# Transposing the token-major SwiGLU blocks: on TensorE, or by DMA in two planes of 16-bit halves

## The chip, the cores and the metric

One core of a Trainium2 chip runs the kernel. The metric is the device time of one execution in microseconds (us), taken as the median of several runs. A profile of one execution stands beside it.

The engines that matter here: PE (TensorE) for matmuls and transposes, ACT (ScalarE), DVE (VectorE), SP (SyncE), which issues nearly all DMAs, and the DMA queue behind SP. Every engine works through its own instructions in order.

## The reference, cut to what matters

```
def _swiglu(t, w_gate, w_up, w_down):
    return (jax.nn.silu(t @ w_gate) * (t @ w_up)) @ w_down

for l in range(DEPTH):                                  # DEPTH = 2
    f = _swiglu(_rmsnorm(h, ffn1_pre_g[l]), ffn1_w_gate[l], ffn1_w_up[l], ffn1_w_down[l])
    h = h + 0.5 * _rmsnorm(f, ffn1_post_g[l])
    ...                                                 # three attentions, gated and merged
    f = _swiglu(_rmsnorm(h, ffn2_pre_g[l]), ffn2_w_gate[l], ffn2_w_up[l], ffn2_w_down[l])
    h = h + 0.5 * _rmsnorm(f, ffn2_post_g[l])
```

The input `x` is 1 x 512 x 1024 in float32; the hidden width `D_FF` is 2816, 22 tiles of 128. So there are four SwiGLU layers, named a0, c0, a1 and c1 in the kernel (a and c are the first and second of a decoder layer).

## The kernel before

Every float32 factor is split into a high and a low part (`split`: an ACT cast makes `wh`, a DVE subtraction makes `wl`), and a product is three matmuls (`mm3`, L202 to L206): high by high, high by low, low by high.

Of the 22 hidden tiles 16 lie in two chunks (`ci`) of 8 tiles. For each chunk, gate and up are computed in `token_products`, as a product of 2 x 2 blocks that needs seven smaller products instead of eight (`n`, in the order 0, 2, 1, 3, 4, 5, 6). In these, tokens are the output's partitions ("token-major"): `token_product` has the activations as the stationary operand and weights of 512 columns as the moving one, four steps `kk` of two groups of three matmuls, 24 matmuls of 128x512. The down products of a chunk (`products`, `product`) are of the same kind, with the hidden values as activations, and these must have the hidden dimension in the partitions. So the finished blocks of the hidden values have to be transposed.

A block of gate times up is finished after the up products n = 1, 4, 5 and 6; it is 128 tokens by 1024 values (two groups of tokens by 512 hidden values). `turn` transposes it in the product that follows, at its step `kk` 2: eight PE transposes of 128x128 into two PSUM banks (L800), and two ACT copies of 128x512 out of them (L802) into the rows of `hr`, which `hidden_rows` gives. That makes 4 blocks x 2 chunks x 4 layers = 32 turns.

`PLAN` (L1635) writes the order of the products of a layer out by hand: seven gate products of chunk 0 (G0), a slot, seven up products (U0), seven gate products of chunk 1 (G1), seven up products (U1), then the fourteen down products with the plain hidden tiles 18 to 21 (`gates`, `ups`) between them. So turns fall in two places of a layer: where U0 goes over into G1, and where U1 goes over into the down products.

Other steps that the prediction follows:

- the weights of a product come in two units of 128x1024 (two `kk` each): a fetch of 512 KB by SP (`BlockUnit.fetch`, issue L296), for some products a DVE difference of two blocks (L326), the ACT cast (L181) and the DVE low part (L182); the `wh` and `wl` rings have four buffers each, which is two products;
- `first_factor` makes the split activations `aha`, `ala` of a down product from `hr`, with differences of its blocks in `asa`;
- evictions of a token product out of PSUM: L775 (ACT) for n = 2 and 3, L777 and L779 (DVE) for the others; L746 (ACT) carries the sum of n = 0 over to the banks of n = 1 before that product begins;
- `tmp` gives a [128, 512] float32 tile from a ring of five buffers (`f32t`), and the tag `rs` has one buffer of [128, 1024] float32.

The tile framework orders the instructions of each engine and sets the waits; `tc.keep_in_program_order` ties an instruction to its place among the others that are tied on its engine.

Of the kernel before, what the change touches and what calls it, by code (L numbers as in the profile page):

```python
# [9 lines left out]
F32 = mybir.dt.float32  # L10
F32R = mybir.dt.float32r
BF16 = mybir.dt.bfloat16
AF = mybir.ActivationFunctionType
ALU = mybir.AluOpType
AX = mybir.AxisListType
# [2 lines left out]
P = 128  # L18
# [4 lines left out]
def kernel(  # L23
# [38 lines left out]
    nc = tc.nc  # L62
    _, S, D = x.shape
# [3 lines left out]
    ND = D // P  # L67
# [7 lines left out]
    FC = 8  # L75
# [12 lines left out]
    ident = cst.tile([P, P], F32, name="ident")  # L88
    make_identity(nc, ident)
    ident16 = cst.tile([P, P], BF16, name="ident16")  # L90
    eps_t = cst.tile([P, 1], F32, name="eps_t")
    nc.vector.memset(eps_t[:], D * EPS)
    one_t = cst.tile([P, 1], F32, name="one_t")
    nc.vector.memset(one_t[:], 1.0)
    causal16 = cst.tile([P, P], BF16, name="causal16")
    sel = cst.tile([104, NH], F32, name="sel")

    def tmp(name):
        return sb.tile([P, S], F32, tag="f32t", bufs=5, name=name)
# [3 lines left out]
    def stile(shape, tag, name, dt=F32R):  # L103
        return sb.tile(shape, dt, tag=tag, bufs=BUFS[tag], name=name)
# [4 lines left out]
    def pbank(tag, name):  # L109
        return ps.tile([P, S], F32, tag=tag, bufs=4, name=name)  # L110
# [67 lines left out]
    def split(h_ap, l_ap, src, scale=None, later=False):  # L178
# [4 lines left out]
        else:  # L183
            both = [nc.scalar.activation(h_ap, src, AF.Copy, scale=scale)]  # L184
            make = lambda: nc.vector.scalar_tensor_tensor(l_ap, src, scale, h_ap.bitcast(F32), ALU.mult, ALU.subtract)  # L185
# [7 lines left out]
    def sigmoid_neg(t, z, c):  # L193

        b, minus = nbgate[:, c[0], c[1]:c[1] + 1], bgate[:, c[0], c[1]:c[1] + 1]
        nc.scalar.activation(t, z, AF.Abs, bias=b)
        nc.scalar.activation(t, t, AF.Exp, scale=-1.0)
        nc.scalar.activation(t, t, AF.Ln, bias=one_t[:])  # L198
        nc.vector.scalar_tensor_tensor(t, z, minus, t, ALU.max, ALU.add)  # L199
        nc.scalar.activation(t, t, AF.Exp, scale=-1.0, bias=minus)  # L200

    def mm3(pt, lh, ll, rh, rl, start, stop, free=False):  # L202

        nc.tensor.matmul(pt, lh, rh, start=start, stop=False, skip_group_check=free)  # L204
        nc.tensor.matmul(pt, lh, rl, start=False, stop=False, skip_group_check=free)  # L205
        nc.tensor.matmul(pt, ll, rh, start=False, stop=stop, skip_group_check=free)  # L206
# [271 lines left out]
    def rstd(st, a, b=None):  # L478

        s, m, y, w = st[:, a:a + 1], st[:, 3:4], st[:, 4:5], st[:, 5:6]  # L480
        if b is None:
            nc.scalar.activation(y, s, AF.Ln, bias=eps_t[:])
            nc.vector.tensor_scalar(m, s, D * EPS, None, ALU.add)
# [118 lines left out]
    def ffn(l, src, wg, wu, wd, dst, name, spare, parked, plan, aside=None):  # L602
# [4 lines left out]


        hid, st = {}, {}
        hr = {}  # L610
        f0 = NC * FC
        tags = ["q"] * 2 + ["o"] * 4
        act = lambda k, c=FULL: quad_act(src.us)(k, c)
# [1 line left out]
        def hidden_rows(i):  # L615
            if i not in hr:
                hr[i] = stile([P, FC // 2, S], ("k", "tri")[i // 2], f"hr{name}_{i}", F32)
            return hr[i]
# [114 lines left out]
        def in_product(n):  # L733
            if n in (0, 1, 6):
                i, j = ((0, 0), (0, 1), None, None, None, None, (1, 1))[n]
                return [block(i, j, part) for part in range(2)]
            return st["u", n]

        def token_product(ci, up, n, uns):

            nm = f"{name}{'gu'[up]}_{ci}_{n}"
            if n in (0, 1, 2):
                st["c", n] = [pbank("z" if n == 0 else "mm", f"pw{nm}_{e}") for e in range(2)]
            if n == 1:
                for e in range(2):
                    nc.scalar.copy(st["c", 1][e][:], st["c", 0][e][:])  # L746
            if n == 0:
                if not up:
                    st["s", ci] = {}
            pts = st["c", SUM[n]]  # L750
            h, l = in_product(n)
            opens, ends = n in (0, 2), n in (1, 4, 6)
            for un in uns:
                for k in range(un.nk):
                    kk = un.k0 + k
                    for e in range(2):
                        c = slice(e * P, (e + 1) * P)
                        mm3(pts[e][:], h[:, kk, c], l[:, kk, c], un.h[:, k], un.l[:, k], opens and kk == 0,
                            ends and kk == ND // 2 - 1, free=True)
                        yield 3 * S * PE_US  # L760
                    if kk == ND // 2 - 2:
                        yield from turn("z")
            if n == 0:
                return
            q = TO[n]
            g = st["s", ci]
            if not up and q not in g:
                g[q] = stile([P, FC // 2, S // 2], "f", f"s{name}_{ci}_{q[0]}{q[1]}", F32)[:]
            g = g[q]
            r = hidden_rows(2 * ci + q[1])[:, :, HALVES[q[0]]] if up else g  # L770
            for e in range(2):
                p = pts[e][:].rearrange("p (f q) -> p f q", f=2)
                re, ge = r[:, 2 * e:2 * e + 2], g[:, 2 * e:2 * e + 2]
                if n in (2, 3):
                    nc.scalar.copy(re, p)  # L775
                elif n in (4, 5):
                    nc.vector.tensor_tensor(re, re, p, ALU.add)  # L777
                elif up:
                    nc.vector.tensor_tensor(ge, p, ge, ALU.mult)  # L779
                else:  # L780
                    nc.scalar.activation(re, p, AF.Silu)
            if n in (4, 5):
                if up:
                    nc.vector.tensor_tensor(g, r, g, ALU.mult)
                else:
                    nc.scalar.activation(r, r, AF.Silu)
            if up and n in (1, 4, 5, 6):
                st["turn"] = (f"{nm}", g, r)

        def turn(tag):  # L790

            nm, g, r = st.pop("turn", (None, None, None))
            if nm is None:
                return
            g = g.rearrange("p f q -> p (f q)")
            for b in range(2):
                pt = pbank(tag, f"ht{nm}_{b}")
                for f in range(2):
                    for e in range(2):
                        nc.tensor.transpose(pt[:, (2 * f + e) * P:(2 * f + e + 1) * P],  # L800
                                            g[:, e * S + (2 * b + f) * P:][:, :P], ident[:])
                nc.scalar.copy(r[:, 2 * b:2 * b + 2], pt[:].rearrange("p (f q) -> p f q", f=2))  # L802
                yield 0.4

        def token_products(ci, up):

# [37 lines left out]
        def product(ci, n, uns):  # L844
            if n == 0 and ci == 0:
                RINGS["o"] = 2
                dst.begin()
            if n < 6:
                first_factor(ci, n + 1)
            if n in (0, 1, 2):  # L850
                st["b", SUM[n]] = [pbank("z", f"pd{name}_{ci}_{n}_{e}") for e in range(2)]
            pts = st["b", SUM[n]]
            if n == 1 and ci:
                for e in range(2):
                    nc.scalar.copy(pts[e][:], dst.fs[e][:, HF[0]])
            h, l = st["a", ci, n]
            opens, ends = n in (0, 2) or (n == 1 and not ci), n in (1, 4, 6)
            for un in uns:
                for k in range(un.nk):
                    kk = un.k0 + k  # L860
                    for e in range(2):
                        c = slice(e * P, (e + 1) * P)
                        mm3(pts[e][:], h[:, kk, c], l[:, kk, c], un.h[:, k], un.l[:, k], opens and kk == 0,
                            ends and kk == FC // 2 - 1, free=True)
                        yield 3 * S * PE_US
                    if kk == FC // 2 - 2:
                        yield from turn("mm")
            if n == 0:
                return
            i, hf = TO[n]  # L870
            for e in range(2):
                f = dst.fs[2 * i + e][:, HF[hf]]
                if n == 1:
                    nc.scalar.copy(f, st["b", 0][e][:])
                    nc.vector.tensor_tensor(f, f, pts[e][:], ALU.add)
                elif ci == 0 and n in (2, 3, 6):
                    nc.scalar.copy(f, pts[e][:])
                else:
                    nc.vector.tensor_tensor(f, f, pts[e][:], ALU.add)
# [767 lines left out]

    wps, wsb = pbank("z", "warm"), tmp("warm").bitcast(BF16)
    nc.vector.memset(wsb[:, 0:S], 0.0)
    mc = None  # L1650
    for l in LAYERS:
        i, mn = 3 * l, []
# [44 lines left out]
```

## Time and profile before

| | |
|---|---|
| median of 3 runs | 2390.12 us (2388.59 to 2391.15) |
| the profiled execution's own time | 2389.31 us |
| its span in the profile | 2387.6 us |
| granted TensorE clock, mean | 0.998 |
| PE busy | 2370.0 us |
| DVE busy | 1844.2 us |
| ACT busy | 1425.1 us |
| GpSimd busy | 75.1 us |
| DMA, mean | 142 GB/s |

Busy time is the time in which an engine has an instruction in work. Matmuls are pipelined and their ends are modelled, so a busy PE is not the same as PE at its peak. In a group of instructions, the figures behind the count are busy time in us and the mean duration of one in ns; behind the second bar stands the idle time just before them and what ended it. In a timeline line the first number is the start in us from the start of the span, the second the length. In a view of windows each engine has its busy time in the stretch, with the number of its instructions, then come the granted clock, the busy share of the DMA engines and their rate.

### The profile page before, as it was taken

To read this page: it belongs to the slowest core of one execution; us is meant where nothing else is said; L and a number is where in the kernel's file an instruction comes from. 1 tells how busy PE (TensorE), PEld (TensorE's weight loads), DVE (VectorE), ACT (ScalarE), POOL (GpSimd) and SP (SyncE) were. 2 spreads that over 40 slices of the span, in tenths; PEclk is the share of its full clock that TensorE was granted. 3 is DMA by queue.
4 is the path that set the end of the run, shared out by engine and by line. 5 is a ranking of instruction groups with operands and counts; after the bars stand their busy time and mean duration, and the time that the engine had idled before them with its cause. 6 is when DMAs were issued, how large, how long until landed. Compare 5 with 4: busy or idle time off the path is not lost.

```text
span 2387.6 us, 31555 instructions
## 1 busy us (share of the span) xinstructions
PE 2370.0 (99%) x11975; PEld 2006.6 (84%) x11975; DVE 1844.2 (77%) x2414; ACT 1425.1 (60%) x2250; POOL 75.1 (3%) x134
## 2 busy tenths in 40 slices
PE   9999999999999999999999999999999999999998
PEld 7888889888888888888888888888888888888887
DVE  8878877577777688788788788766777767887885
ACT  6655555576766555555655554656777664655554
POOL 1000000000111000000000000000001100000000
PEclk9999999999999999999999999999999999999999
DMA  6554455223323655444645554542323235555444
GB/s 205 184 150 158 142 189 147 80 82 87 89 72 106 195 175 175 144 158 157 206 140 167 150 176 156 187 116 71 98 71 97 80 115 198 164 176 154 154 140 153
DMA packets 232173, 338.23 MB, mean 142 GB/s; under 512 B 10683, under 2 KB 125395, under 8 KB 232021
## 3 DMA queue, kind: packets, MB, share of 16 engines
q1 hardware_dynamic: 231924, 336.18, 44.3%
q8 instruction: 94, 1.54, 0.3%
q14 instruction: 59, 0.48, 0.1%
q0 software_dynamic: 96, 0.03, 0.0%
HBM read 319.39 MB, written 16.78 MB: 141 GB/s over the span
## 4 chain that ended last, share of the span: by engine, by line
PE 89%; DVE 5%; DMA 3%; ACT 2%; issue 1%; SPq 0%; POOL 0%; DVEq 0%; ACTq 0%
PE pg L205 3%; PE pg L204 3%; PE pg L206 3%; PE pda L205 3%; PE pda L206 3%; PE pda L204 3%; PE pdc L205 3%; PE pdc L206 2%; PE pdc L204 2%; PE pb L206 1%; PE pb L205 1%; PE pb L204 1%; PE pq L205 1%; PE pq L204 1%; PE pq L206 1%
## 5 line engine op out<-in xcount | busy, mean ns | idle before, releaser
L204 PE MATMUL pg<-us_a,wh_wg 128*128 128x512 f32 x384 | 150.9, 393 | 0.0
L205 PE MATMUL pg<-us_a,wh_wg 128*128 128x512 f32 x384 | 149.8, 390 | 0.0
L206 PE MATMUL pg<-us_a,wl_wg 128*128 128x512 f32 x384 | 149.7, 390 | 0.0
L205 PE MATMUL pda<-wl_da,aha 128*128 128x512 f32 x224 | 87.6, 391 | 0.6 <-DVE wl_da L182 0.5
L205 PE MATMUL pdc<-wl_dc,ahc 128*128 128x512 f32 x224 | 87.5, 391 | 0.3 <-DVE wl_dc L182 0.3
L204 PE MATMUL pda<-wh_da,aha 128*128 128x512 f32 x224 | 87.4, 390 | 0.0
L204 PE MATMUL pdc<-wh_dc,ahc 128*128 128x512 f32 x224 | 87.4, 390 | 0.0
L206 PE MATMUL pda<-wh_da,ala 128*128 128x512 f32 x224 | 87.2, 389 | 0.0
L206 PE MATMUL pdc<-wh_dc,alc 128*128 128x512 f32 x224 | 87.2, 389 | 0.0
L206 PEld LDWEIGHTS pg<-us_a,wl_wg 128*128 128x128 f32 x384 | 72.1, 188 | 15.2
L204 PEld LDWEIGHTS pg<-us_a,wh_wg 128*128 128x128 f32 x384 | 72.1, 188 | 14.1
L205 PEld LDWEIGHTS pg<-us_a,wh_wg 128*128 128x128 f32 x384 | 72.2, 188 | 14.1
L182 DVE TENSOR_TENSOR wl_dc<-raw_dc,wh_dc 128x1024 fp32r<-128x1024 f32 x50 | 61.1, 1223 | 29.3 <-ACT wh_dc L181 29.1
L181 ACT CAST wh_dc<-raw_dc 128x1024 fp32r<-128x1024 f32 x50 | 52.6, 1053 | 43.9 <-PE pdc L206 15.1
L182 DVE TENSOR_TENSOR wl_da<-raw_da,wh_da 128x1024 fp32r<-128x1024 f32 x50 | 61.1, 1223 | 22.3 <-ACT wh_da L181 22.0
L181 ACT CAST wh_da<-raw_da 128x1024 fp32r<-128x1024 f32 x50 | 52.7, 1055 | 39.3 <-PE pda L206 15.0
L185 DVE SCALAR_TENSOR_TENSOR wl_wg<-raw_wg,wh_wg 128x1024 fp32r<-128x1024 f32 x48 | 58.4, 1220 | 21.6 <-ACT wh_wg L184 21.6
L199 DVE SCALAR_TENSOR_TENSOR ga<-pg,bgate,ga 128x512 f32<-128x512 f32 x48 | 35.9, 747 | 49.5 <-ACT ga L198 49.5
L181 ACT CAST wh_uc<-raw_uc 128x1024 fp32r<-128x1024 f32 x44 | 46.3, 1053 | 43.5 <-PE pwc1u L206 10.3
L181 ACT CAST wh_ua<-raw_ua 128x1024 fp32r<-128x1024 f32 x44 | 46.2, 1053 | 34.3 <-PE pwa1u L206 10.3
L184 ACT ACTIVATE wh_wg<-raw_wg 128x1024 fp32r<-128x1024 f32 x48 | 50.5, 1057 | 24.0 <-PE pv L1088 11.7
L182 DVE TENSOR_TENSOR wl_uc<-raw_uc,wh_uc 128x1024 fp32r<-128x1024 f32 x44 | 53.7, 1220 | 14.3 <-ACT wh_uc L181 14.2
(655 smaller groups left out, 8044.4 us busy)
## 6 DMA issues: line engine op xcount, KB each, us to landing
raw_da<-in_ffn_w_down_dram SPq DMA_DIRECT2D x66, 512.0 KB, 4.6
raw_dc<-in_ffn_w_down_dram SPq DMA_DIRECT2D x66, 512.0 KB, 5.3
raw_ga<-in_ffn_w_gate_dram SPq DMA_DIRECT2D x52, 512.0 KB, 3.9
raw_ua<-in_ffn_w_up_dram SPq DMA_DIRECT2D x52, 512.0 KB, 3.9
raw_gc<-in_ffn_w_gate_dram SPq DMA_DIRECT2D x52, 512.0 KB, 3.8
raw_uc<-in_ffn_w_up_dram SPq DMA_DIRECT2D x52, 512.0 KB, 3.8
raw_wg<-in_w_gate_dram SPq DMA_DIRECT2D x48, 512.0 KB, 3.5
raw_wo<-in_w_out_dram SPq DMA_DIRECT2D x24, 512.0 KB, 3.6
```

The lines of the kernel that those rows point to most:

```text
L181: both = [nc.scalar.copy(h_ap, src)]
L182: make = lambda: nc.vector.tensor_tensor(l_ap, src, h_ap.bitcast(F32), ALU.subtract)
L184: both = [nc.scalar.activation(h_ap, src, AF.Copy, scale=scale)]
L185: make = lambda: nc.vector.scalar_tensor_tensor(l_ap, src, scale, h_ap.bitcast(F32), ALU.mult, ALU.subtract)
L199: nc.vector.scalar_tensor_tensor(t, z, minus, t, ALU.max, ALU.add)
L204: nc.tensor.matmul(pt, lh, rh, start=start, stop=False, skip_group_check=free)
L205: nc.tensor.matmul(pt, lh, rl, start=False, stop=False, skip_group_check=free)
L206: nc.tensor.matmul(pt, ll, rh, start=False, stop=stop, skip_group_check=free)
```

## The change

The turn of a block no longer uses PE. A float32 word is taken as two 16-bit halves:

- two ACT copies split the block's words into two planes of 128x1024 halves (`th`, both in `tmp` tiles), tied to step `kk` 1 of the product after the one that finished the block;
- two DMA transposes, issued by SP and tied to step `kk` 3 of the same product, turn each plane, in eight groups of 128 columns, into a plane `tr`. For the blocks n = 1 and 5 both planes lie in the one buffer of `rs`, for n = 4 and 6 in two `tmp` tiles;
- two ACT copies join the planes in `hr`, each writing every second half-word, tied to steps `kk` 0 and 1 of the third product after the one that finished the block (`age` 2).

The list `turns` holds the blocks that are under way; `token_product` and `product` call `turn(kk)` at each step.

```diff
+U16 = mybir.dt.uint16
...
-        hr = {}
+        hr, turns = {}, []
...
-                    if kk == ND // 2 - 2:
-                        yield from turn("z")
+                    turn(kk)
...
             if up and n in (1, 4, 5, 6):
-                st["turn"] = (f"{nm}", g, r)
-
-        def turn(tag):
-
-            nm, g, r = st.pop("turn", (None, None, None))
-            if nm is None:
-                return
-            g = g.rearrange("p f q -> p (f q)")
-            for b in range(2):
-                pt = pbank(tag, f"ht{nm}_{b}")
-                for f in range(2):
-                    for e in range(2):
-                        nc.tensor.transpose(pt[:, (2 * f + e) * P:(2 * f + e + 1) * P],
-                                            g[:, e * S + (2 * b + f) * P:][:, :P], ident[:])
-                nc.scalar.copy(r[:, 2 * b:2 * b + 2], pt[:].rearrange("p (f q) -> p f q", f=2))
-                yield 0.4
+                turns.append([nm, g, (2 * ci + q[1], q[0]), n in (1, 5), 0, None])
+
+        def turn(kk):
+
+            later = tc.keep_in_program_order
+            for one in turns:
+                nm, g, (row, i), own, age, planes = one
+                if kk == 1 and age == 0:
+                    one[5] = planes = [tmp(f"th{nm}_{h}")[:].bitcast(U16) for h in range(2)]
+                    words = g.rearrange("p f q -> p (f q)").bitcast(U16)
+                    for h, plane in enumerate(planes):
+                        later(nc.scalar.copy(plane, words[:, h::2]))
+                if kk == 3 and age == 0:
+                    one[5] = ([stile([P, 2, 2 * S], "rs", "tr" + nm, U16)[:, h] for h in range(2)] if own else
+                              [tmp(f"tr{nm}_{h}")[:].bitcast(U16) for h in range(2)])
+                    for plane, part in zip(one[5], planes):
+                        later(nc.sync.dma_start_transpose(plane.rearrange("p (r q) -> p r q", q=P), part))
+                if kk in (0, 1) and age == 2:
+                    r = hidden_rows(row)[:].bitcast(U16)
+                    later(nc.scalar.copy(r[:, :, i * S + kk:(i + 1) * S:2].rearrange("p f (e q) -> p e f q", e=2),
+                                         planes[kk].rearrange("p (e f q) -> p e f q", e=2, q=P)))
+                if kk == ND // 2 - 1:
+                    one[4] += 1
+            turns[:] = [one for one in turns if one[4] < 3]
...
-                    if kk == FC // 2 - 2:
-                        yield from turn("mm")
+                    turn(kk)
```

## The prediction

> **What bounds the kernel now.** I read the page first: span, busy shares, the chain that ended last.
>
> ```profile
> span 2387.6 us, 31555 instructions
> PE 2370.0 (99%) x11975; PEld 2006.6 (84%) x11975; DVE 1844.2 (77%) x2414; ACT 1425.1 (60%) x2250; POOL 75.1 (3%) x134
> PE 89%; DVE 5%; DMA 3%; ACT 2%; issue 1%; SPq 0%; POOL 0%; DVEq 0%; ACTq 0%
> ```
>
> TensorE (PE) is busy all the time and carries 89% of the chain. What leaves PE's queue is a gain as long as nothing else becomes late; what delays a PE operand by more than its cover is a loss.
>
> The transposes that go were looked up by their tile, and one of their groups in the timeline of PE:
>
> ```profile
> L800 PE MATMUL hta0u<-ident,sa x64: 270/272/273, 98.1 to 204.6; 128*128 128x128 f32 x64
> L802 ACT COPY hra<-hta0u x16: 586/590/593, 98.7 to 204.9; 128x512 f32<-128x512 f32 x16
> ```
>
> ```profile
> 93.99 0.39 PE L204 MATMUL pwa0u<-wh_ua,uha 128*128 128x512 f32 x1
> ...
> 97.84 0.39 PE L206 MATMUL pwa0u<-wh_ua,ula 128*128 128x512 f32 x1
> 98.07 1.03 PE L800 MATMUL hta0u<-ident,sa 128*128 128x128 f32 x8
> 98.86 0.48 PE L204 MATMUL pwa0u<-wh_ua,uha 128*128 128x512 f32 x1
> 99.18 0.40 PE L205 MATMUL pwa0u<-wl_ua,uha 128*128 128x512 f32 x1
> 99.41 0.39 PE L206 MATMUL pwa0u<-wh_ua,ula 128*128 128x512 f32 x1
> ...
> 130.19 0.39 PE L204 MATMUL pwa0g<-wh_ga,uha 128*128 128x512 f32 x1
> ```
>
> Matmuls overlap; they start 0.226 us apart (93.99 to 97.84 is 17 steps). From 97.84 to 99.41 are 1.57 us, of which three matmuls are 0.68: a group of eight transposes costs PE 0.89 us.
>
> Then I read how full the other engines are where those groups lie, first gate/up block to second (four groups) and up block to down (four):
>
> ```profile
> core 0: us, PE busy (x) PEld busy (x) DVE busy (x) ACT busy (x) POOL busy (x), PEclk, DMA share, GB/s
> 94.00:130.00 36.00, 35.67 (x174) 29.53 (x173) 29.68 (x32) 18.99 (x24) 0.00 (x0) 1.00 0.52 151
> 174.50:210.50 36.00, 35.82 (x173) 29.34 (x173) 26.55 (x27) 20.99 (x26) 0.00 (x0) 1.00 0.39 130
> ```
>
> ACT has 15 to 17 us free in each 36, and DMA about half.
>
> **Removed.** 64 transposes in each of four SwiGLU layers are 32 groups: 32 x 0.89 = 28.5 us of PE, 3.56 us in each of eight stretches. 64 ACT copies of 512 elements go with them. This is the whole of what can be won.
>
> **Added on ACT.** Per group two split copies and two join copies of 128x1024, all on ACT. The trace has no 16-bit copy; nearest are these:
>
> ```profile
> 126.57 1.06 ACT L746 COPY pwa0g<-pwa0g 128x512 f32<-128x512 f32 x2
> 128.40 1.05 ACT L181 CAST wh_ga<-tga 128x1024 fp32r<-128x1024 f32 x1 [0.76 <-ACT pwa0g L746]
> 130.39 0.59 ACT L775 COPY sa<-pwa0g 128x512 f32<-128x512 f32 x1 [0.94 <-PE pwa0g L206]
> 180.89 1.05 ACT L181 CAST aha<-hra 128x1024 fp32r<-128x1024 f32 x1
> 181.84 1.05 ACT L181 CAST wh_ua<-raw_ua 128x1024 fp32r<-128x1024 f32 x1
> 182.79 0.59 ACT L775 COPY hra<-pwa0u 128x512 f32<-128x512 f32 x1
> ```
>
> Casts of 1024 elements that follow each other start 0.95 us apart. If a copy went by bytes, 1024 halves would be 512 words: two L746 copies in 1.06, some 0.5 each. I take 0.95, since split and join have as many elements as the cast; the ends are 0.5 and 1.05. Stretch one then holds 18.99 - 4 x 1.06 + 16 x 0.95 = 29.9 us of ACT in 32.4 us: it fits as a sum, but ACT works in order, so the order decides.
>
> **Walk of stretch one**, t counted from 93.99, a product of 24 matmuls 5.43 us. Products: up n=3 from 0, n=4 5.4, n=5 10.9, n=6 16.7 (two matmuls of the next gate block go first), gate n=0 22.2, n=2 27.2 to 32.6, then n=1. Weight casts cannot be pulled ahead, as each waits for the product that frees its buffer:
>
> ```profile
> ACT wh_ua L181 <- PE pwa0u L206: 5.0, 4, 1.7
> ACT wh_ga L181 <- PE pwa0u L206: 4.7, 3, 2.3
> ```
>
> In the changed program's ACT queue the cast for gate n=2, first half, comes when up n=6 is half done, at 19.7. Behind it stand, with no wait for PE that is still open: a join of turn 1, the splits of turn 4, a cast, the splits of turn 5, two casts, the joins of turn 4, the splits of turn 6, two casts, a join of turn 5: with the first 16 steps of 0.95, to 34.9. Then two evictions (L775 before) and only then the copies that carry the sum of n=0 over to n=1 (L746 before). In the old queue those stood ahead of the evictions: the row at 126.57 is t = 32.6, and n=1 began at about 130.2 without a wait. Now the first of them ends at 34.9 + 2 x 0.48 + 0.59 = 36.5; PE, at full pace done with n=2 at 32.6, restarts at 36.7. A hole of 4.1 us, where 3.56 was saved. Without any delay on ACT the new order alone would leave 1.5 (both evictions and a copy after n=2's end).
>
> **Added on the DMA queue.** Per group two transposes of a 128x1024 plane of halves (256 KB), issued by SP behind a wait for the split, in the same queue as all weights. Nothing in the trace transposes by DMA. Its nearest rows:
>
> ```profile
> q1 hardware_dynamic: 231924, 336.18, 44.3%
> raw_ga<-in_ffn_w_gate_dram SPq DMA_DIRECT2D x52, 512.0 KB, 3.9
> gsave<-ga SPq DMA_DIRECT2D x16, 256.0 KB, 2.1
> gb<-gsave SPq DMA_DIRECT2D x16, 256.0 KB, 4.0
> bta<-in_ffn_w_down_dram SPq DMA_DIRECT2D x8, 512.0 KB, 4.8
> ```
>
> By bytes: 336.18 MB in 44.3% of 2387.6 us is 318 GB/s, so a plane holds the queue 0.82 us. By packets: 0.443 x 2387.6 x 16 / 231924 = 73 ns each; a plane read in rows of 128 halves is 1024 packets over 16 engines, 4.7 us. A plane cannot be under the first, since its bytes move; the second may be passed if the scattered side is slower. No row is nearer to one end, so I take the middle, 2.8 us. It lands 2.1 (the same bytes from SBUF) + 2.0 = 4.1 us after its issue, close to the 4.0 of the slower 256 KB row; the next one 2.8 later.
>
> In stretch one the second split of turn 5 takes the buffer that holds the first plane of turn 4. That plane is split by 22.6 and lands at 26.8, where the split would have begun at 25.4: ACT slips 1.5 us, the hole grows to 5.6. Stretch one: 5.6 - 3.56 = +2.0 us.
>
> **Stretch two**, t from 174.55. SP issues there, one behind the other, turn 4's planes, turn 5's first, two weight fetches, turn 5's second (behind its split) and only then the four fetches that make the down block's product n=2. Before, these were out by t = 31:
>
> ```profile
> 200.42 0.50 SPq L296 DMA_DIRECT2D bta<-in_ffn_w_down_dram  x1
> 205.03 0.37 SPq L296 DMA_DIRECT2D raw_da<-in_ffn_w_down_dram  x1
> 205.44 0.46 SPq L296 DMA_DIRECT2D bta<-in_ffn_w_down_dram  x1
> 210.90 1.05 ACT L181 CAST wh_da<-bta 128x1024 fp32r<-128x1024 f32 x1 [1.29 <-DVE bta L326]
> ```
>
> ```profile
> L182 DVE TENSOR_TENSOR wl_dc<-raw_dc,wh_dc 128x1024 fp32r<-128x1024 f32 x50 | 61.1, 1223 | 29.3 <-ACT wh_dc L181 29.1
> ```
>
> Turn 4 is split by 24.6: its planes land at 28.7 and 31.5, turn 5's first at 34.3, two fetches (1.6 each by bytes) at 37.5, turn 5's second at 40.3, the first bta at 41.9. Difference, cast and low part (1.22 + 1.05 + 1.22) make it 45.4. PE, after up n=6, down n=0 and n=1 and 41 matmuls of a plain gate pair that the new order puts first, wants it at 41.8. With the second half a little late too, the hole is 4.5: 4.5 - 3.56 = +0.9 us. DVE's wait for ACT adds nothing further: its queue has about 6 us free in stretch one, and PE's hole widens that.
>
> **Sum.** 4 x (2.0 + 0.9) = +12 us on the profiled execution's 2389.31 (1.7 around the span; the median of three is 2390.12, 0.8 more): **2401 us**.
>
> PE's holes could cost clock as well. The granted clock, 1.00 in the stretches above, is under that only where PE starts or waits:
>
> ```profile
> 0.00:20.00 20.00, 16.51 (x89) 11.49 (x90) 12.44 (x27) 13.96 (x24) 1.89 (x8) 0.91 0.87 290
> ```
>
> Holes of 4 to 6 us once in 90 us I take as free. The Trainium skill (TensorE: Matmul & The Clock Gate, Why this matters for your kernels) says that an idle gap over some 3 us lets the clock fall to half for a window of 3.4 us; by it, as an estimate, each of eight holes could add up to 1.7 us, 2415 in all. No run here shows it.
>
> **Rivals.** *Planes move by bytes (0.82 us).* Then no split or fetch waits for a plane: stretch one is 4.1 - 3.56 = +0.5, stretch two the full -3.56, 4 x -3.0 = -12 us, **2377 us**, faster. Against the forecast's +12 the sign turns near 1.8 us a plane. For it: the half-free queue; against: rows of 256 bytes, scattered. The Trainium skill (DMA: Bandwidth & Descriptors, Latency and other measured facts) gives 261 GB/s for transposing DMAs: an estimate of 1.0 us a plane, so this side.
>
> *Planes move by packets (4.7 us, landing 6.0).* Stretch one: turn 4's planes land at 28.7 and 33.4, and ACT slips 4.2 (hole 8.3); turn 5's second, behind turn 6's and two fetches, lands near 55, the cast for gate n=4 stands behind its join, and PE waits another 8: +12.5. Stretch two: down n=2's weights come 11.5 late: +8. 4 x 20.5 = +82, **2471 us**. The Trainium skill (VectorE: DVE Perf Modes, The three transpose paths) has 1309 ns for one 128x128 transpose on the DMA crossbar against 390 on TensorE and advises TensorE; eight in a row, an estimate of 10.5 us a plane, would be worse still.
>
> *16-bit copies go by bytes (0.5 us) and planes too.* ACT is then never late, only the order's 1.5 us remain in stretch one: -28.5 + 4 x 1.5 = -22, **2367 us**. Against it: no row of ACT shows time following bytes.
>
> **Numbers.** Forecast (planes of 1.8 to 4 us) 0.38, its own range 2390 to 2445; by bytes 0.30; by packets or worse 0.25; cheap copies 0.07. A measurement of this kernel tells about 0.2% (4.8 us) from no change. Faster takes 0.27 of the second and all of the last but 0.01: 0.33; same 0.11 (the low edge of the forecast and what is left of the second); slower 0.56. The range 2372 to 2465 leaves out about 0.06 below and 0.14 above.
>
> **What would show it.** Right: no PE transpose by ident under the token products; PE idle of about 5 us ahead of gate n=1, ended by the carry copy, in each of four layers, and of about 4 ahead of down n=2, ended by the low part of its weights; planes landing about 4 us after issue. Wrong: landings near 2 us and PE without the second hole (first rival); ACT idle in long waits for DMA in front of joins (second); copies near 0.5 us (third). If the hole ahead of gate n=1 is missing with copies near 1 us, my walk of ACT's order is wrong.

## The result, and the profile after

The changed kernel takes 2417.22 us (median of four runs, 2414.65 to 2421.91) against 2389.72 for the kernel before: 1.0115 times as long, 95% interval 1.0102 to 1.0128. It is 27.5 us slower. The forecast was +12.

The new lines make the line numbers of the changed kernel a little higher: the weight casts are L182, their low parts L183, the three matmuls of a product L205 to L207, the carry copies L747, the splits L799, the transposing DMAs L804, the joins L807, the fetches of the block weights L297.

The page of the changed kernel, with the rows shown of before:

```profile
span 2416.4 us, 31245 instructions
...
PE 2355.6 (97%) x11719; PEld 1987.2 (82%) x11719; DVE 1840.5 (76%) x2414; ACT 1523.6 (63%) x2314; POOL 74.4 (3%) x134
...
q1 hardware_dynamic: 299508, 352.97, 48.1%
...
PE 80%; DVE 6%; DMA 6%; ACT 5%; issue 3%; SPq 0%; POOL 0%; DVEq 0%; ACTq 0%
```

PE has 256 instructions less and is busy 14.4 us less, but its share of the chain fell from 89% to 80%: it waits now. What it waits for (in total, times, longest):

```profile
PE pwa1g L205 <- ACT pwa1g L747: 7.0, 1, 7.0
PE pwc0g L205 <- ACT pwc0g L747: 6.9, 1, 6.9
PE pwa0g L205 <- ACT pwa0g L747: 6.7, 1, 6.7
PE pwc1g L205 <- ACT pwc1g L747: 6.6, 1, 6.6
PE pdc L205 <- ACT wh_dc L182: 5.3, 2, 2.9
PE pda L205 <- ACT wh_da L182: 4.7, 2, 2.6
PE pda L206 <- DVE wl_da L183: 3.0, 5, 1.1
```

The first four rows are the forecast's hole ahead of gate n=1, ended by the carry copy, one in each layer: 27.2 us in all. The next two are the holes ahead of down n=2, also one in each layer, of 2.1 to 2.9 us: the forecast had 4.5 there, ended by the low part of the weights, and it is their cast that ends them. The stretches that the prediction looked at:

```profile
94.00:130.00 36.00, 34.56 (x150) 27.73 (x149) 30.43 (x33) 24.18 (x26) 0.00 (x0) 1.00 0.69 175
174.50:210.50 36.00, 36.00 (x161) 29.70 (x160) 27.95 (x28) 24.55 (x27) 0.00 (x0) 1.00 0.51 138
```

ACT rose from 19 and 21 us to 24 in each and is still a third idle. No sum overran; the order did. ACT's timeline around the first hole, which runs from 129.60 to 136.27:

```profile
127.28 2.55 ACT L807 COPY hra<-tra0u 128x1024 uint16<-128x1024 uint16 x2
129.71 1.98 ACT L799 COPY tha0u<-sa 128x1024 uint16<-128x1024 uint16 x2
131.59 1.99 ACT L182 CAST wh_ga<-tga 128x1024 fp32r<-128x1024 f32 x2
133.48 1.33 ACT L807 COPY hra<-tra0u 128x1024 uint16<-128x1024 uint16 x1
134.68 1.04 ACT L775 COPY sa<-pwa0g 128x512 f32<-128x512 f32 x2
135.63 1.07 ACT L747 COPY pwa0g<-pwa0g 128x512 f32<-128x512 f32 x2
136.62 3.85 ACT L807 COPY hra<-tra0u 128x1024 uint16<-128x1024 uint16 x3
```

While PE stands, ACT works through splits, casts, a join and the evictions, and only then does the carry copies of 1.07 us that PE waits for. None of this waits for PE any more.

The granted clock shows a second price. Windows of PE alone around that hole (PE busy, instructions, granted clock, DMA share, GB/s):

```profile
126.37:129.79 3.42, 3.23 (x15) 1.00 0.31 34
129.79:133.20 3.41, 0.00 (x0) 1.00 1.10 311
133.20:136.61 3.41, 0.34 (x1) 0.50 0.76 155
136.61:140.03 3.42, 3.42 (x9) 0.50 0.98 252
140.03:143.44 3.41, 3.41 (x17) 1.00 0.25 96
```

At each of the four holes the clock goes to half for 6.8 us, two windows; the first of them begins while PE still stands. In a full window at half clock PE does 9 matmuls, at full clock 17. PE is busy for 16.5 us of these four stretches, which at full clock would be about half of that: 8.3 us lost in the profiled execution. The mean granted clock was 0.994 in it and 0.991 to 0.992 in the other three, so there the loss may be larger.

The new instructions, looked up by line (durations min/median/max in ns; the last row is the transposes' time from issue to landing):

```profile
L799 ACT COPY tha0u<-sa x16: 1031/1042/1047, 101.8 to 215.1; 128x1024 uint16<-128x1024 uint16 x16
```

```profile
L807 ACT COPY hra<-tra0u x16: 1327/1352/1381, 112.7 to 230.3; 128x1024 uint16<-128x1024 uint16 x16
```

```profile
L804 SPq DMA_TRANSPOSE tra0u<-tha0u x16: 1231/1242/3173, 107.5 to 224.7; - x16
DMA to landing us min/median/max: 3.0/3.3/7.9
```

A split costs what a cast costs, as taken. A join, which writes every second 16-bit word, is 1.35 long; two in a row take 2.55 (ACT's timeline at 127.28), so they start 1.20 apart and not 0.95. The queue's row gives the planes' time, if all that the row grew by is theirs: (48.1% x 2416.4 - 44.3% x 2387.6) / 64 = 1.6 us each, under the 2.8 taken.

And one wait was not foreseen at all. SP's timeline in stretch two, a join from ACT's timeline, and what SP waited for:

```profile
208.97 1.25 SPq L804 DMA_TRANSPOSE tra0u<-tha0u  x1
211.18 2.26 SPq L297 DMA_DIRECT2D raw_da<-in_ffn_w_down_dram  x2
218.35 1.24 SPq L804 DMA_TRANSPOSE tra0u<-tha0u  x1
219.64 1.09 SPq L297 DMA_DIRECT2D bta<-in_ffn_w_down_dram  x2
```

```profile
216.96 1.36 ACT L807 COPY hra<-tra0u 128x1024 uint16<-128x1024 uint16 x1
```

```profile
SPq L804 <- ACT fa L881: 5.7, 1, 5.7
```

The transpose at 218.35 is turn 5's second plane. ACT's join of the first plane runs from 216.96 to 218.32. `[stile(..., "rs", ...)[:, h] for h in range(2)]` asks for a tile once per plane, and "rs" has one buffer: the second plane gets the buffer of the first and waits until it has been joined (the view names the next copy on ACT, L881). The fetches of the down weights stand behind it on SP: `bta` goes out at 219.64, at 200.42 and 205.44 before.

**Where the 27.5 us lie.** The matmuls other than the turns' are 11,719 in all kernels. Every layer is cut at three places of PE's order, the 75th, the 403rd and the 778th of these matmuls, counted from the layer's first up matmul; in the changed kernel's first layer they start at 90, 175 and 265 us. Stretch one lies between the first two cuts, stretch two between the last two. The table has their time summed over four layers, the rest, and the sum, from the first of these matmuls to the last (us, profiled executions; `plain_turn` and the last two are experiments below):

| kernel | one | two | rest | sum |
|---|---|---|---|---|
| before | 314.5 | 358.9 | 1705.2 | 2378.6 |
| plain_turn | 300.4 | 342.0 | 1705.7 | 2348.2 |
| changed | 336.2 | 361.1 | 1710.1 | 2407.4 |
| after_dve | 305.4 | 356.4 | 1708.4 | 2370.2 |
| tile_dve | 300.1 | 349.0 | 1706.9 | 2356.0 |

Against before, stretch one is +21.7 (forecast +8), stretch two +2.2 (forecast +3.6), the rest +4.9 (forecast nothing), 28.8 together in these two executions.

### The profile page after: what moved, and what is told of

It reads as the page before. It is cut to its first block, busy times and chain, and to the rows that moved or that the text cites. A ratio compares the mean times of both kernels' runs of the same rounds, so it can differ in the third digit from the quotient of the medians.

```text
span 2416.4 us, 31245 instructions
## 1 busy us (share of the span) xinstructions
PE 2355.6 (97%) x11719; PEld 1987.2 (82%) x11719; DVE 1840.5 (76%) x2414; ACT 1523.6 (63%) x2314; POOL 74.4 (3%) x134
## 3 DMA queue, kind: packets, MB, share of 16 engines
q1 hardware_dynamic: 299508, 352.97, 48.1%
## 4 chain that ended last, share of the span: by engine, by line
PE 80%; DVE 6%; DMA 6%; ACT 5%; issue 3%; SPq 0%; POOL 0%; DVEq 0%; ACTq 0%
PE pg L206 4%; PE pg L205 4%; PE pg L207 4%; PE pda L207 2%; PE pda L206 2%; PE pda L205 2%; PE pdc L207 2%; PE pdc L205 2%; PE pdc L206 2%; PE pb L205 1%; PE pb L206 1%; PE pb L207 1%; PE pq L206 1%; PE pq L205 1%; PE pq L207 1%
## 5 line engine op out<-in xcount | busy, mean ns | idle before, releaser
L205 PE MATMUL pg<-us_a,wh_wg 128*128 128x512 f32 x384 | 151.1, 394 | 0.0
L207 PE MATMUL pg<-us_a,wl_wg 128*128 128x512 f32 x384 | 149.9, 390 | 0.0
L205 PE MATMUL pdc<-wh_dc,ahc 128*128 128x512 f32 x224 | 86.9, 391 | 5.3 <-ACT wh_dc L182 5.3
L205 PE MATMUL pda<-wh_da,aha 128*128 128x512 f32 x224 | 86.9, 391 | 4.7 <-ACT wh_da L182 4.7
L207 PE MATMUL pda<-wh_da,ala 128*128 128x512 f32 x224 | 86.9, 391 | 1.2 <-DVE ala L183 1.2
L207 PE MATMUL pdc<-wh_dc,alc 128*128 128x512 f32 x224 | 86.9, 391 | 1.2 <-DVE alc L183 1.2
L207 PEld LDWEIGHTS pg<-us_a,wl_wg 128*128 128x128 f32 x384 | 72.1, 188 | 15.2
L205 PEld LDWEIGHTS pg<-us_a,wh_wg 128*128 128x128 f32 x384 | 72.2, 188 | 14.1
L183 DVE TENSOR_TENSOR wl_dc<-raw_dc,wh_dc 128x1024 fp32r<-128x1024 f32 x50 | 61.0, 1223 | 28.5 <-ACT wh_dc L182 28.2
L182 ACT CAST wh_dc<-raw_dc 128x1024 fp32r<-128x1024 f32 x50 | 52.4, 1052 | 40.7 <-PE pdc L207 14.0
L183 DVE TENSOR_TENSOR wl_da<-raw_da,wh_da 128x1024 fp32r<-128x1024 f32 x50 | 61.0, 1222 | 21.5 <-ACT wh_da L182 21.2
L182 ACT CAST wh_da<-raw_da 128x1024 fp32r<-128x1024 f32 x50 | 52.5, 1054 | 36.1 <-PE pda L207 14.3
L182 ACT CAST wh_uc<-raw_uc 128x1024 fp32r<-128x1024 f32 x44 | 46.3, 1052 | 43.2 <-PE pwc1u L207 10.3
L182 ACT CAST wh_ua<-raw_ua 128x1024 fp32r<-128x1024 f32 x44 | 46.2, 1051 | 35.5 <-PE pwa1u L207 10.3
L183 DVE TENSOR_TENSOR wl_ga<-raw_ga,wh_ga 128x1024 fp32r<-128x1024 f32 x40 | 48.3, 1221 | 21.1 <-ACT wh_ga L182 20.9
```

What stands on the lines that cost most here:

```text
L182: both = [nc.scalar.copy(h_ap, src)]
L183: make = lambda: nc.vector.tensor_tensor(l_ap, src, h_ap.bitcast(F32), ALU.subtract)
```

## The experiments

Each is compared with the kernel before on the same chip; behind a time stand its ratio to that and the 95% interval. They ran in four groups on different chips, where the kernel before took 2389.6 to 2391.1 us, so times of different groups compare to about 2 us. The changed kernel is at 2417.2, 1.0115. Theory: the holes are set by ACT's order and by the join-to-transpose wait, and the clock adds to them. Rivals: the planes' time on the queues; ACT's load as such.

**plain_turn: the size of the gain**

```diff
-  (splits, transposing DMAs, joins)
+                if kk == 1 and age == 0:
+                    r = hidden_rows(row)[:, :, HALVES[i]]
+                    for b in range(2):
+                        later(nc.scalar.copy(r[:, 2 * b:2 * b + 2], g[:, 2 * b:2 * b + 2]))
```

> A turn is two plain ACT copies of the block into the hidden rows, at its old place in the second kk of the product behind it; no split, no transposing DMA, no join, and no TensorE transpose. The block is left untransposed. What is asked is the size of the first term, 28.5 us of TensorE time (32 turns of 0.89 us). If that time lay on the path, the kernel takes 2389.7 - 28.5 = 2361 us (2358 to 2365). Were part of the transposes hidden beside other work, it stays above 2365.

Measured 2361.06 us (0.9877, 0.9863 to 0.9892): 28.7 us under the 2389.8 beside it. The first term of the sum holds, and all of it was on the path.

**one_tile: without the unforeseen wait**

```diff
-                    one[5] = ([stile([P, 2, 2 * S], "rs", "tr" + nm, U16)[:, h] for h in range(2)] if own else
+                    one[5] = ([t[:, h] for t in [stile([P, 2, 2 * S], "rs", "tr" + nm, U16)] for h in range(2)] if own else
```

> In the change, the two planes of turns 1 and 5 are asked for as two tiles of a tag with one buffer, so the second transposing DMA waits until the join of the first plane has read it. Here both planes are halves of one tile, of the same bytes. Theory (holes set by ACT's order and that wait): the second transpose goes out 1.3 us behind the first, the fetches of the down weights behind it on SP's queue are not held, and the holes ahead of down n=2 (about 4 us in each of four layers) go; ACT is ahead by some 2.5 us in the first stretch, so that the hole ahead of gate n=1 shrinks from 6.7 to about 4 us. Sum 4 x (4 + 2.7) = 27, so 2390 us with the half-clock stretches still there, 2377 if they go as well. Rival (it is the transposing DMAs' own time, or the load they put on ACT): the same transposes and copies take the same time, 2413 to 2418.

Measured 2407.08 us (1.0072, 1.0057 to 1.0087). The wait costs something, 10 us and not 27. The clock took part of the gain: 12 windows at half clock and no longer 8, with PE busy for 33.8 us of them against 16.5. The holes ahead of gate n=1 went from 6.6 to 7.0 to 5.8 us: as turn 5's planes come together, both joins, no longer one, stand ahead of the carry copies. The holes ahead of down n=2 stayed, 2.2 to 2.5 us, now ended by a DVE addition that stands behind ACT's copies.

**carry_early: the copies that PE waits for, moved up**

```diff
-            if n in (0, 1, 2):
-                st["c", n] = [pbank("z" if n == 0 else "mm", f"pw{nm}_{e}") for e in range(2)]
-            if n == 1:
+            for m in {0: (0,), 2: (2, 1), 1: ()}.get(n, ()) if ci and not up else {0, 1, 2} & {n}:
+                st["c", m] = [pbank("z" if m == 0 else "mm", f"pw{nm[:-1]}{m}_{e}") for e in range(2)]
+            if n == (2 if ci and not up else 1):
```

> In the second chunk's gate the carry copies of the first product's banks are issued at the start of product 2 and no longer at that of product 1, so that they stand ahead of product 2's evictions, of the last turn's splits or behind them, on ACT. Nothing else differs from the changed kernel. Theory: the four holes of 6.6 to 7.0 us ahead of gate n=1 shrink below 3 us, and the half-clock stretches behind them (4 x 3.4 us lost) go: 2417 - 4 x 6 - 13.7 = 2379 us (2374 to 2386). Rival (the planes' landing is late, and each hole moves to the next product): the holes come back ahead of the next eviction, 2405 to 2418.

Measured 2424.09 us (1.0149, 1.0132 to 1.0165): a miss of 45 us, on the rival's side and past it. The holes did shrink, to 2.1 to 3.1 us, but the wait moved. ACT's timeline:

```profile
130.47 1.04 ACT L747 COPY pwa0g<-pwa0g 128x512 f32<-128x512 f32 x2
131.45 1.35 ACT L807 COPY hra<-tra0u 128x1024 uint16<-128x1024 uint16 x1
135.97 1.33 ACT L807 COPY hra<-tra0u 128x1024 uint16<-128x1024 uint16 x1 [3.17 <-DMA tra0u<-tha0u]
```

Behind the copies ACT now reaches the second join of turn 5 before its plane has landed, since its transpose could only go out after the first join; casts and evictions wait behind it, and PE stalls again (1.1 to 1.4 us) further on. Eleven windows at half clock follow the shorter holes of both stretches; PE is busy for 37.4 us of them, against 16.5 in the changed kernel.

**both: the two edits together**

> Both edits: the planes of turns 1 and 5 in one tile, and the carry copies of the second chunk's gate issued early. Theory: holes of both stretches and the half-clock stretches go, and the gain of TensorE is left: 2390 - 28.5 plus a few us of small holes, 2363 to 2370 us. Rival (each edit takes away the same wait): no better than the better of the two alone.

Measured 2382.25 us (0.9971, 0.9959 to 0.9983): faster than before, but 12 us over the range's top. The edits need each other: -10 and +7 us alone, -35 together.

**three: a third copy moved up**

```diff
+            if n == 1:
+                for e in range(2):
+                    nc.scalar.copy(dst.fs[e][:, HF[0]], st["b", 0][e][:])
             h, l = st["a", ci, n]
...
                 if n == 1:
-                    nc.scalar.copy(f, st["b", 0][e][:])
                     nc.vector.tensor_tensor(f, f, pts[e][:], ALU.add)
```

> The kernel with both edits, and a third: in the down products, the ACT copy of the first product's banks into the output rows is issued at the start of product 1 and no longer at its end, where it stood behind joins and casts and held the DVE addition for which down n=2 waits. Theory (the holes come of where short copies stand behind joins in ACT's order): the four holes of 1.9 to 2.5 us ahead of down n=2 go, with the half-clock windows behind three of them: 2382 - 8 - 4 = 2370 us (2366 to 2375). Rival (the down weights' fetches, queued behind the transposing DMAs, come late anyway): the hole is set by the cast of the fetched weights, and no more than 0.5 us each goes: 2379 to 2383.

Measured 2380.06 us (0.9957, 0.9942 to 0.9972). The rival's range: the hole is now ended by the low half of the down weights (PE waits 8.1 us in all for `wl_da` and `wl_dc`).

**both_no_dma: no transposing DMA**

```diff
-                if kk == 3 and age == 0:
-                    one[5] = (...)
-                    for plane, part in zip(one[5], planes):
-                        later(nc.sync.dma_start_transpose(...))
```

> The kernel with both edits, but without the transposing DMAs: each join reads the split planes themselves (so the block is not transposed). Splits and joins keep their places and times on ACT. It parts what is left between both edits (2382 us) and a plain turn (2361 us). Theory A (queue: the planes' time on SP's and the DMA queues and the joins' wait for them): 2361 to 2368 us. Theory B (ACT's work: four copies of 1.04 to 1.35 us a turn in place of two of 0.59, in an order that other engines wait for): 2376 to 2383 us.

Measured 2375.86 us (0.994, 0.9923 to 0.9956): at the edge of theory B. Of the 21 us between `both` and a plain turn the DMAs and the waits for them have about 6, ACT's copies and their order about 15.

**junk_dma: the DMAs alone**

```diff
+            junk = stile([P, 2, 2 * S], "rs", "jk" + nm, mybir.dt.uint16)
+            for b in range(2):
+                tc.keep_in_program_order(nc.sync.dma_start_transpose(
+                    junk[:, b].rearrange("p (r q) -> p r q", q=P),
+                    g.bitcast(mybir.dt.uint16)[:, b * 2 * S:(b + 1) * 2 * S]))
```

> The kernel before, TensorE turns and all, with 64 transposing DMAs added behind the turns at the place where the change has them, each of a contiguous half of the block's words (junk) into a tile that nobody reads. It prices the DMAs alone: SP's issue of 1.24 us each, their time on the DMA queue, and what is queued behind them. If they cost nothing by themselves: 2389 to 2393 us. If the planes' time on the queue is what the change pays: 21 us and more, 2410 to 2420 us.

Measured 2400.93 us (1.0043, 1.0028 to 1.0058): between the two ranges, +10 us. Of the 8.3 us that the profiled execution shows by the cut above, 7.0 lie in stretch two (stretch one -0.2), where the down weights' fetches stand behind transposes on SP.

**ladder: the clock by itself**

```diff
-                for e in range(2):
+                for e in [0, 1] * ({"a0": 4, "c0": 5, "a1": 6, "c1": 8}[name] if ci and not up else 1):
```

> The kernel before, with the second chunk's carry copies done 4, 5, 6 and 8 times over in the four layers, which makes a hole ahead of gate n=1 of its own length in each. The slack ahead of it is 2.6 us and a pair takes 1.03 us, so the holes come to about 0.5, 1.5, 2.6 and 4.6 us, 9 us together. Theory (the granted clock is set for windows of 3.41 us on a fixed grid, and a window with TensorE idle for more than about 1.85 us is followed by one at half clock): the third and fourth hole are followed by half-clock windows, one or two each, the first two by none; 2389.7 + 9 + 2 x 1.7 to 4 x 1.7 = 2402 to 2406 us. Rival (an idle gap of over 3 us is what drops the clock): only the fourth is, 2400 to 2402 us. The clock's records tell the two apart, the time hardly.

Measured 2409.61 us (1.0079, 1.0064 to 1.0094), above both ranges, with holes of 0.6, 3.0, 4.0 and 5.9 us, longer than expected by 4.3 in all. Windows of PE, on the grid on which the clock changes, for the last three holes (PE busy, instructions, clock, DMA share, GB/s):

```profile
973.50:976.91 3.41, 1.52 (x7) 1.00 0.38 141
976.91:980.33 3.42, 2.30 (x10) 1.00 0.59 168
980.33:983.74 3.41, 3.41 (x17) 1.00 0.48 144
1318.23:1321.65 3.42, 1.79 (x8) 1.00 0.44 149
1321.65:1325.06 3.41, 1.05 (x5) 1.00 0.51 154
1325.06:1328.47 3.41, 3.41 (x10) 0.50 0.52 154
2168.18:2171.59 3.41, 0.00 (x0) 1.00 0.36 86
2171.59:2175.00 3.41, 0.94 (x2) 0.50 0.62 204
2175.00:2178.42 3.42, 3.42 (x9) 0.50 0.06 21
```

The 3.0 us hole lies across two windows, idle 1.88 and 1.13: no drop. Of the 4.0 us hole 2.36 fall into one window: one window at half. The 5.9 us hole empties one and most of the next: two. As the third hole came out longer than 3 us, it no longer tells theory from rival. Another run does: in `three` a hole of 2.2 us that lies within one window drops the clock:

```profile
1054.01:1057.42 3.41, 1.21 (x5) 1.00 1.19 237
1057.42:1060.84 3.42, 3.42 (x10) 0.50 1.08 274
```

So the clock goes by the window and not by the hole's length. Over all 16 kernels, without the start and the end of the span, every window at full clock with 1.9 us idle or more was followed by one at half, and none with under 1.3 was; between, both occur (1.88 with no drop above and 1.85 in `junk_dma`, 1.3 to 1.85 with a drop in `after_pool`). When a second one follows is not settled: in `one_tile` one did behind a half-clock window with 0.65 us idle.

**after_pool, three_pool, three_pool2: joins, or joins and splits, on GpSimd**

```diff
-                    later(nc.scalar.copy(r[:, :, i * S + kk:(i + 1) * S:2]...
+                    later(nc.gpsimd.tensor_copy(r[:, :, i * S + kk:(i + 1) * S:2]...
```

`three_pool2` does the same with the splits' `nc.scalar.copy(plane, ...)`.

> The changed kernel with one edit: the joins are done by GpSimd and no longer by ACT. The wait of the second transposing DMA for the first join stays. Theory (the holes ahead of gate n=1 come of the joins that stand ahead of the carry copies in ACT's order): three joins of 1.2 us and ACT's wait for a plane leave ACT's way, so that the four holes of 6.6 to 7.0 us go to 2 us or less and the half-clock windows with them: 2417 - 4 x (5 + 2) = 2389 us (2383 to 2396). Rival (GpSimd's copies take longer than ACT's 1.35 us, or take time from DVE's): 2405 us and more.

> The kernel with all three edits, and the joins on GpSimd. Without the transposing DMAs both edits still stood 15 us above a plain turn, which is put down to ACT's work: 64 joins of 1.2 us off ACT should bring 6 to 12 us of it: 2368 to 2374 us. Rival (the late fetches set what is left, as the kernel before with transposes added shows +10 us): 2376 to 2381 us. If GpSimd slows DVE down: over 2381 us, with longer DVE rows.

> The kernel with all three edits, splits and joins on GpSimd: ACT does nothing for a turn any more. Theory: 2365 to 2372 us, what is left being the fetches behind the transposing DMAs. Rival: GpSimd takes so long for a split and a join that the planes come too late for the down products' factors, or it slows DVE down: 2380 us and more.

Measured 2400.86 (1.0045, 1.0028 to 1.0062), 2417.36 (1.0117, 1.01 to 1.0134) and 2427.21 us (1.0155, 1.014 to 1.0171). The first, between its theory and its rival, took 16 of the 27.5 us back and has no hole ahead of gate n=1 above 0.9 us; the others, on the side of their rivals, lost 37 and 47 against `three`. A join takes GpSimd 1.34 to 2.45 us, and with the same work DVE is busy longer: 1839.8 us in `three`, 1888.9 and 1928.7 here. From the timelines of GpSimd (POOL), DVE and PE in `three_pool`:

```profile
120.16 4.14 POOL L807 COPY hra<-tra0u 128x1024 uint16<-128x1024 uint16 x2 [5.24 <-DMA tra0u<-tha0u]
120.76 2.33 DVE L183 TENSOR_TENSOR wl_ga<-tga,wh_ga 128x1024 fp32r<-128x1024 f32 x1
125.05 3.69 POOL L807 COPY hra<-tra0u 128x1024 uint16<-128x1024 uint16 x2 [0.75 <-DMA tra0u<-tha0u]
125.24 2.29 DVE L183 TENSOR_TENSOR wl_ga<-raw_ga,wh_ga 128x1024 fp32r<-128x1024 f32 x1
127.59 0.50 PE L206 MATMUL pwa0g<-wl_ga,us_x 128*128 128x512 f32 x1 [3.30 <-DVE wl_ga L183]
129.68 1.21 DVE L183 TENSOR_TENSOR wl_ga<-raw_ga,wh_ga 128x1024 fp32r<-128x1024 f32 x1
```

Beside the joins the DVE subtraction that makes a low part takes 2.3 us, without one 1.21, and the second of them ends a hole of 3.3 us in PE. Of the 608 such subtractions the 37 that lie for more than half of their time beside a join take 1.91 us on average, the others 1.23. Why `three_pool` is 16 us slower than `after_pool`, with the same copies on GpSimd, was not worked out.

**three_dve, after_dve, tile_dve: joins on DVE**

The same edit with `nc.vector.tensor_copy`: on the kernel of three edits, on the changed kernel alone, and on `one_tile`.

> The kernel with all three edits, and the joins on DVE. ACT is freed as with GpSimd, but DVE is busy for 77% of the span and the holes left in the second stretches wait for its low halves of the weights. Theory: what ACT gains DVE loses, 2376 to 2386 us; if DVE copies 16-bit words much faster than 1.2 us, 2370 to 2376 us.

> The changed kernel with one edit: the joins are done by DVE (0.75 us each there, as the run with three edits and DVE joins showed) and no longer by ACT (1.35). The second transposing DMA's wait for the first join stays; the order built for ACT puts the carry copies ahead of the evictions again. Theory (the holes ahead of gate n=1 come of the joins in ACT's order; what GpSimd's joins left of 11 us over the kernel before was GpSimd's slowing of DVE): the four holes and their half-clock windows go, the second stretches stay near the change's, 2417 - 4 x 7.5 = 2387 us (2380 to 2393). Rival (the false wait alone holds the planes back so far that the holes stay wherever the joins are done): 2400 us and more.

> The changed kernel with two edits: joins on DVE, and the two planes of turns 1 and 5 in one tile; the carry copies and the down products' copies stay where the change has them. Theory: without the false wait a few us more go in both stretches: 2375 to 2382 us, level with the kernel of all three edits and DVE joins (2377). Rival (the moved copies did the work there): 2384 us and more.

Measured 2376.67 (0.9942, 0.9927 to 0.9957), 2380.88 (0.9956, 0.9939 to 0.9973) and 2365.80 us (0.9893, 0.9879 to 0.9908). A join takes DVE 0.75 us, the row of `tile_dve` by line:

```profile
L807 DVE COPY hra<-tra0u x16: 735/753/772, 116.0 to 218.9; 128x1024 uint16<-128x1024 uint16 x16
```

The first two lie in their theories' ranges; the third is 9 us under its own. `after_dve` decides the question: with the joins off ACT, and the unforeseen wait still there, the holes ahead of gate n=1 are 1.7 us at most, and stretch one falls by 30.9 of the 35.8 us that the change stood above a plain turn. With the wait gone too, in `tile_dve`, stretch one equals the plain turn's (300.1 against 300.4), although all transposing DMAs are there; no window falls to half clock between the start and the end of the span, and 25 of the 28.7 us come out. It needs neither of the moved copies: with the joins elsewhere, the order built for ACT has the carry copies ahead of the evictions again. So the edit takes the joins' time out of ACT's queue and mends its order at once; these runs do not part the two. With the moved copies (`three_dve`) the kernel is 11 us slower. The PE waits of `tile_dve`, all that come to over 1.5 us in total:

```profile
PE pdc L206 <- DVE wl_dc L183: 5.2, 6, 1.8
PE pda L206 <- DVE wl_da L183: 3.6, 4, 1.5
```

Stretch two still stands 6.9 us over a plain turn, which fits what the DMAs alone add there (7.0 in `junk_dma`).

## Why the prediction was right in its sign and wrong in its size

- **Removed, 28.5 us of PE.** Right: 28.7 by `plain_turn`.
- **Stretch one, +8.** The step that failed: 4 x 2.0 was +21.7, and so 13.7 of the 17 us by which the forecast's +12 (11.6 before rounding) fell short of the 28.8 between the two profiled executions. The place was right (gate n=1, behind the carry copies, in ACT's order), and `after_dve` shows that the hole goes when the joins leave ACT. Two sizes were not right. The *hole*, 5.6 by the walk, is 6.6 to 7.0, 4.8 us more over four layers; some 4.0 of these come of the four joins ahead of it in each layer, which are 1.20 apart and not 0.95. The *clock*, "Holes of 4 to 6 us once in 90 us I take as free", costs 8.3 us. These two make 13.1. The Trainium skill (TensorE: Matmul & The Clock Gate, Why this matters for your kernels) was right where I set it aside: the clock does fall, for windows of 3.41 us. Its rule of an idle gap over some 3 us does not fit as it stands: a hole of 3.0 us across two windows was followed by no half-clock window, one of 2.2 within a window was. The estimate from it, 13.6 us, had eight drops of 1.7; there were four of 2.1.
- **ACT's slip for late planes, 1.5 us.** Near in size for another reason: ACT waited 1.26 us ahead of turn 1's second join and 0.51 ahead of turn 5's split in the first layer. The first comes of the one-buffer wait, not of the queue.
- **Planes on the queue, 2.8 us and landing at 4.1.** Too much: 1.6 us by the queue's row, landing 3.3 in the median. By the prediction's own turning point of 1.8 us that should have made the kernel faster. It did not, because the joins' length, the clock and the one-buffer wait, all at nothing or too little in the sum, hold the holes open; this error hid part of the others, and so the right sign is in part luck. The Trainium skill (DMA: Bandwidth & Descriptors, Latency and other measured facts) has 261 GB/s for transposing DMAs; a plane of 256 KB in 1.6 us is some 160 GB/s here, in a queue that also carries weights. The Trainium skill (VectorE: DVE Perf Modes, The three transpose paths) gave an estimate of 10.5 us a plane; here it is 1.6.
- **Stretch two, +3.6.** Near in size (+2.2), not in cause. The walk had one hole of 4.5 us in each layer, with the weights late by the planes' queue time. There are holes of 2.1 to 2.9 us ahead of down n=2 and smaller ones beside them. Three causes show, in each case by the cut: the DMAs ahead of the fetches (7.0 alone, by `junk_dma`), the one-buffer wait (7.5, `after_dve` less `tile_dve`), and the joins on ACT (6.4, `both` at 355.4 less `tile_dve`, of which some 5 are half-clock windows; 4.0 by `three` less `three_dve`). They come to 18.5 to 20.9, where 19.1 stand over the plain turn. The sizes are rough: each depends on which other edits are in, and `both` was profiled in an execution 3.6 us above its median.
- **The rest, 0.** It is +4.9 in the profiled execution, spread thin; what it is stays open.
- **Rivals.** By bytes (2377): its plane of 0.82 us was nearer than mine, its time not. By packets (2471): a plane took 1.6 us on average, not 4.7. Cheap copies (2367): ACT's copies are not cheap. DVE's joins of 0.75 us come nearer, and with those and without the one-buffer wait the kernel is at 2366; that the numbers meet is chance, since that rival had planes by bytes and four copies of 0.5 us on ACT.

## What to carry to other kernels

Work that leaves the bounding engine lands in another engine's order; ask not whether it fits in that engine's idle time but which short operation, waited for by the bounding engine, now stands behind it, and try the engine that does the copy fastest before moving anything else. A tile asked for inside a loop over parts, from a tag with one buffer, makes the parts wait for each other's readers. Holes of a few microseconds in TensorE have a second price in the granted clock.

## What the runs showed of the hardware that was not expected

- The granted clock changes on a fixed grid of 3.41 us: a window with some 1.9 us idle or more is followed by one at half. Where a hole lies on the grid decides, so a hole of 2.2 us (`three`) can cost clock where one of 3.0 (`ladder`) does not.
- The same 128x1024 copy of 16-bit words with a stride of two on the written side takes 0.75 us on DVE, 1.35 on ACT and 1.34 to 2.45 on GpSimd (in `three_pool` 2.05 on average where DVE was busy for over 90% of the copy, 1.36 where it was not); with the stride on the read side ACT takes 1.04.
- GpSimd's copies lengthen DVE's work: 64 joins on GpSimd (which is busy 122 us longer with them) added 49 us to DVE's busy time; a subtraction of 1.22 us took up to 2.3 beside them.
- A transposing DMA holds SP's queue for 1.24 us, against 0.37 for the shortest fetch of weights in the same timeline, and for up to 4.1 us in the changed kernel.
